# A gMLP and stick-breaking trunk in fp32r: two more pairs of columns five tile pairs wide, and a mixing in wider products

## The chip, the cores and the metric

The kernel runs on one core of a Trainium2 chip. Its engines are TensorE (PE in the profile, its weight loads PEld), VectorE (DVE), ScalarE (ACT), GpSimd (POOL) and SyncE (SP). The metric is the device time of one execution, in microseconds: the median of several runs. A profiled execution gives, beside its own time, a trace of every instruction.

## The reference

Two layers over a sequence of 256 tokens with 2048 channels (16 tiles of 128 channels, two tiles of 128 tokens).

```python
h = x
for i in range(DEPTH):                       # DEPTH = 2
    hn = rms_norm(h, norm_g[i])
    if i % 2 == 0:                           # layer a: gMLP, width 4096
        proj = hn @ a_w_in                   # 2048 x 12288: u | v | gate
        u, v = split(gelu(proj[:, :8192]));  zg = proj[:, 8192:]
        v = rms_norm(v, a_v_norm_g)
        mixed = tril(a_w_s) applied to v by chunks of 128 tokens, + a_b_s   # 16 groups of 256 channels
        y = (u * mixed * silu(zg)) @ a_w_out # 4096 x 2048
    else:                                    # layer b: stick-breaking attention, 16 heads of 128
        q, k, v, zg = split(hn @ b_w_in)     # 2048 x 8192
        y = (attention(q, k, v) * silu(zg)) @ b_w_out
    h = h + y
return rms_norm(h, final_g)
```

Nearly all arithmetic is in the four projections. All is float32.

## The kernel before, in words

**Split products.** A float32 factor is split into a high part in the type fp32r and a low part, the rest. A product then takes three matmuls: high by high, high by low, low by high (`terms`, L119 to L121). The left factor (activations, two token tiles) is split once and stays on chip. The weights come from memory, two k tiles (128x1024) at a time, and `cut` splits them: ScalarE copies the high part (L114), VectorE subtracts it for the low part (L115). Five pairs of such tiles can be in work (`wspl`).

**Pairs.** `Pair` computes two blocks of 512 columns at once. Of its k tiles, `ks` pairs are done with seven products of 2x2 blocks instead of eight (Winograd's form), the rest plainly in `column(0)` and `column(1)`. With k halves i and columns j the weights are tiles `b00`, `b01`, `b10`, `b11` in the program's names (b11, b12, b21, b22 in the code). The seven products are the blocks p1, p5, p6, p2, p7, p3, p4 in this order, each over `ks` tiles in groups of two (`qk0_p50` is block p5 of pair qk0, its first group). With `ks` = 5 the third group is a half one, of one tile (128x512): `p12`, `p52` and so on. Between the blocks VectorE forms differences and sums of the weight tiles (L275, L300), and POOL issues DMAs that add one tile onto another (`plus`, L280). The matching sums of the left factor are made once per layer by `sums`, for the fifth tile by `fifth`.

Before the change the v pairs (v0 to v6, layer a) and the first q/k pair (qk0, layer b) have `ks` = 4, as the gate/u pairs do (gu0 to gu7); the later pairs of layer b have 5. The fifth tiles of b00 and b01 lie in a pool of their own, those of b10 and b11 in the three buffers that also hold the loads of the plain columns (`wraw`).

**What sets the order.** The tile framework arranges each engine's instructions by its own estimate of time; the Python order, and a queue of small works that `tick` takes from, give it its input. Each engine then runs its list strictly in that order. A pair's second column is interleaved with the next pair's head: `run`, and by hand for the passage from o2 (the last pair of layer a's output) to qk0. All loads of weights are issued by SyncE (L221), in its order. In the text, the lead of a group is the time from the end of its low part's subtraction to the first product that reads it.

**The mixing** (`mixing`, one block of 512 v columns for each gu pair) splits the masked mixing matrix (`wh`, `wl`) and the normed v (`vh`, `vl`), and multiplies them by groups of 256 columns: for each token tile and group three products of 256 columns (L580 to L582), 12 in all, and a multiplication by the gain per token tile (L584).

**Attention's constants** are made when qk0 is under way: `mones`, `nu` and `one` by VectorE copies, `never` by a VectorE memset and a select on POOL; `n1_r`, layer b's norm factor, is computed on POOL too (L97).

Of the kernel before, what the change touches and what calls it, by code (L numbers as in the profile page):

```python
# [29 lines left out]
def trunk_kernel(ctx: ExitStack, tc: tile.TileContext, x, xt, gcols, wst, a_w_in, a_v_norm_g,  # L30
# [187 lines left out]

    def load(out, in_):

        ins = ins_of(nc.sync.dma_start(out, in_))  # L221
# [325 lines left out]
    with ExitStack() as lg:  # L547
# [5 lines left out]
        def mixing(b, pair):  # L553
# [15 lines left out]
            mixed[b] = []  # L569
            for t in range(NT):  # L570
                vh = pb.tile([P, CB], F32R, tag="vh", name=f"vh{b}_{t}")
                vl = pb.tile([P, CB], F32R, tag="vl", name=f"vl{b}_{t}")
# [1 line left out]
                nc.scalar.activation(vh, vs, AF.Identity, scale=rv[:, t:t + 1])
                nc.vector.scalar_tensor_tensor(vl, vs, rv[:, t:t + 1], f(vh), op0=ALU.mult, op1=ALU.subtract)
                mp = ps_ms.tile([P, CB], F32, tag="ms", name=f"mix{b}_{t}")
                for j in range(GPB):
                    o = mp[:, j * GD:(j + 1) * GD]
                    sl = slice(j * GD, (j + 1) * GD)
                    nc.tensor.matmul(o, wh[:, j, :], vh[:, sl], start=True, stop=False)  # L580
                    nc.tensor.matmul(o, wh[:, j, :], vl[:, sl], start=False, stop=False)
                    nc.tensor.matmul(o, wl[:, j, :], vh[:, sl], start=False, stop=True)  # L582
                ym = pa.tile([P, CB], F32, tag=f"ym{t}", name=f"ym{b}_{t}")
                nc.vector.tensor_mul(ym, mp, vg)  # L584
                mixed[b].append(ym)

        def evac_gu(b, j, t, bank):
            ym = mixed[b][t]
# [217 lines left out]
    nc.vector.tensor_copy(nu, scr2)  # L806
# [2 lines left out]
    nc.vector.memset(never, 0.0)
# [346 lines left out]
```

## Time and profile before

| | us |
|---|---|
| median of 3 runs (lowest to highest) | 1147.48 (1147.37 to 1147.52) |
| the profiled execution's own time | 1147.16 |
| its span, first to last instruction | 1145.4 |
| TensorE busy | 1134.8 (99%) |
| VectorE busy | 1006.3 (88%) |
| ScalarE busy | 816.6 (71%) |
| bytes moved | 263.69 MB, 230 GB/s on average |

A row of the timeline reads: start and duration in us, engine, line, operation, out<-in by the program's names without their numbers, shape, and in brackets how long the engine was idle before it and what ended that. `x3` is three instructions in one row. A row of the waits reads: who waited <- for whom, us in total, times, longest. Matmul durations overlap, so the cadence is read from starts. A row of the stretches gives busy time by engine, the granted clock of TensorE, the share of the DMA engines' time and the rate.

### The profile page before, as it was taken

What the parts mean: (1) busy time and instruction counts of PE and PEld (TensorE: products, weight loads), DVE (VectorE), ACT (ScalarE), POOL (GpSimd) and SP (SyncE); (2) the same over time, 40 slices, a digit from 0 to 9 for tenths busy, and PEclk for the clock granted to TensorE, in tenths of its full rate; (3) what the DMA queues carried; (4) which work ended last, traced back from release to release, by engine and by line L of the source; (5) the groups of instructions that cost most, each with busy time, mean ns of one, the idle gap of its engine ahead of it and who ended that gap; (6) DMA issues with size and microseconds to landing.
All of it is one profiled execution on the core that took longest, in us unless ns stands there. A gap on an engine that the chain in (4) does not pass through costs nothing.

```text
span 1145.4 us, 14888 instructions
## 1 busy us (share of the span) xinstructions
PE 1134.8 (99%) x5222; PEld 940.5 (82%) x5222; DVE 1006.3 (88%) x1108; ACT 816.6 (71%) x1072; POOL 94.5 (8%) x101
## 2 busy tenths in 40 slices
PE   9999999999999999999999999999999999999997
PEld 6788888888888888888888888888888888888885
DVE  7988888998999998987988679989889989897995
ACT  7777767767767767856657456788678877886574
POOL 0200010110110110100010000110100101100000
PEclk9999999999999999999999999999999999999999
DMA  9988787786787786677795768687787876837972
GB/s 330 319 274 250 194 262 256 195 270 231 204 258 241 212 257 224 182 236 203 254 270 171 266 201 284 170 268 208 184 283 199 211 228 173 273 87 241 334 225 82
DMA packets 135020, 263.69 MB, mean 230 GB/s; under 512 B 8864, under 2 KB 9376, under 8 KB 134816
## 3 DMA queue, kind: packets, MB, share of 16 engines
q1 hardware_dynamic: 117408, 227.57, 59.1%
q0 software_dynamic: 15728, 31.99, 15.6%
q10 hardware_dynamic: 1808, 3.17, 0.8%
q8 instruction: 41, 0.67, 0.2%
q14 instruction: 35, 0.29, 0.1%
HBM read 258.50 MB, written 4.19 MB: 229 GB/s over the span
## 4 chain that ended last, share of the span: by engine, by line
PE 96%; DMA 1%; ACT 1%; issue 1%; DVE 1%; SPq 0%; POOLq 0%; POOL 0%; ACTq 0%
PE gu_a L121 3%; PE gu_a L120 3%; PE gu_b L121 3%; PE gu_a L119 3%; PE gu_b L120 3%; PE gu_b L119 3%; PE gu_d L121 2%; PE op_acc L121 2%; PE gu_d L120 2%; PE op_acc L119 2%; PE op_acc L120 2%; PE gu_c L121 2%; PE gu_d L119 2%; PE gu_c L120 2%; PE gu_c L119 2%; PE qk_a L121 1%
## 5 line engine op out<-in xcount | busy, mean ns | idle before, releaser
L114 ACT CAST gu_p_hi<-gu_b 128x1024 fp32r<-128x1024 f32 x112 | 115.4, 1052 | 36.1 <-PE gu_c L121 19.7
L115 DVE TENSOR_TENSOR gu_p_lo<-gu_b,gu_p_hi 128x1024 fp32r<-128x1024 f32 x112 | 133.6, 1221 | 5.4 <-ACT gu_p_hi L114 4.9
L115 DVE TENSOR_TENSOR qk_p_lo<-qk_b,qk_p_hi 128x1024 fp32r<-128x1024 f32 (+1 forms) x77 | 80.8, 1075 | 8.3 <-ACT qk_p_hi L114 7.9
L114 ACT CAST gu_hi<-gu_raw 128x1024 fp32r<-128x1024 f32 x64 | 65.9, 1053 | 29.7 <-DMA gu_raw<-in_a_w_in 17.0
L115 DVE TENSOR_TENSOR gu_lo<-gu_raw,gu_hi 128x1024 fp32r<-128x1024 f32 x64 | 76.7, 1218 | 10.1 <-ACT gu_hi L114 10.1
L114 ACT CAST qk_p_hi<-qk_b 128x1024 fp32r<-128x1024 f32 (+1 forms) x77 | 70.4, 934 | 19.0 <-DMA qk_b<-in_b_w_in 4.6
L115 DVE TENSOR_TENSOR v_lo<-v_raw,v_hi 128x1024 fp32r<-128x1024 f32 (+1 forms) x41 | 48.4, 1193 | 21.2 <-ACT v_hi L114 21.0
L114 ACT CAST v_hi<-v_raw 128x1024 fp32r<-128x1024 f32 (+1 forms) x41 | 41.7, 1027 | 28.4 <-DMA v_raw<-in_a_w_in 26.3
L115 DVE TENSOR_TENSOR v_p_lo<-v_b,v_p_hi 128x1024 fp32r<-128x1024 f32 x42 | 50.2, 1220 | 3.3 <-ACT v_p_hi L114 3.1
L114 ACT CAST v_p_hi<-v_b 128x1024 fp32r<-128x1024 f32 x42 | 43.0, 1049 | 9.5 <-PE v_c L121 4.7
L115 DVE TENSOR_TENSOR bv_p_lo<-bv_b,bv_p_hi 128x1024 fp32r<-128x1024 f32 (+1 forms) x42 | 42.6, 1041 | 4.2 <-ACT bv_p_hi L114 4.0
L115 DVE TENSOR_TENSOR bg_p_lo<-bg_b,bg_p_hi 128x1024 fp32r<-128x1024 f32 (+1 forms) x42 | 42.4, 1040 | 4.1 <-ACT bg_p_hi L114 4.0
L114 ACT CAST o_p_hi<-o_b 128x1024 fp32r<-128x1024 f32 (+1 forms) x35 | 33.4, 966 | 16.6 <-PE op_acc L121 11.6
L114 ACT CAST bv_p_hi<-bv_b 128x1024 fp32r<-128x1024 f32 (+1 forms) x42 | 37.2, 908 | 9.6 <-DMA bv_b<-in_b_w_in 3.3
L114 ACT CAST bg_p_hi<-bg_b 128x1024 fp32r<-128x1024 f32 (+1 forms) x42 | 37.2, 907 | 7.9 <-DMA bg_b<-in_b_w_in 2.5
L114 ACT CAST op_hi<-op_raw 128x1024 fp32r<-128x1024 f32 x24 | 25.1, 1053 | 23.6 <-DMA op_raw<-in_a_w_out 10.5
L115 DVE TENSOR_TENSOR o_p_lo<-o_b,o_p_hi 128x1024 fp32r<-128x1024 f32 (+1 forms) x35 | 38.3, 1113 | 3.8 <-ACT o_p_hi L114 3.7
L114 ACT CAST o_hi<-o_raw 128x1024 fp32r<-128x1024 f32 x22 | 23.0, 1052 | 24.3 <-DMA o_raw<-in_a_w_out 23.2
L115 DVE TENSOR_TENSOR o_lo<-o_raw,o_hi 128x1024 fp32r<-128x1024 f32 x22 | 26.7, 1222 | 15.4 <-ACT o_hi L114 15.2
L280 POOL DMA_DIRECT2D gu_b<-in_a_w_in x16 | 19.7, 1228 | 237.7 <-DVE gu_b L275 202.2
L275 DVE TENSOR_TENSOR gu_b<-gu_b,gu_b 128x1024 f32<-128x1024 f32 x32 | 39.0, 1238 | 0.2
L114 ACT CAST qk_hi<-qk_raw 128x1024 fp32r<-128x1024 f32 x26 | 27.1, 1054 | 15.2 <-DMA qk_raw<-in_b_w_in 9.9
(773 smaller groups left out, 3820.0 us busy)
## 6 DMA issues: line engine op xcount, KB each, us to landing
gu_b<-in_a_w_in SPq DMA_DIRECT2D x64, 512.0 KB, 4.8
gu_raw<-in_a_w_in SPq DMA_DIRECT2D x64, 512.0 KB, 5.3
v_raw<-in_a_w_in SPq DMA_DIRECT2D x39, 512.0 KB, 6.0
qk_b<-in_b_w_in SPq DMA_DIRECT2D x32, 512.0 KB, 5.1
qk_raw<-in_b_w_in SPq DMA_DIRECT2D x26, 512.0 KB, 5.4
v_b<-in_a_w_in SPq DMA_DIRECT2D x24, 512.0 KB, 5.6
op_raw<-in_a_w_out SPq DMA_DIRECT2D x24, 512.0 KB, 5.4
o_raw<-in_a_w_out SPq DMA_DIRECT2D x22, 512.0 KB, 4.9
```

What stands on the lines that cost most here:

```text
L114: nc.scalar.copy(hi[:, sl], raw[:, sl])
L115: low[0] = nc.vector.tensor_sub(lo[:, sl], raw[:, sl], f(hi[:, sl]))
L119: nc.tensor.matmul(acc, lh, hi, start=first, stop=False, skip_group_check=True)
L120: nc.tensor.matmul(acc, lh, lo, start=False, stop=False, skip_group_check=True)
L121: nc.tensor.matmul(acc, ll, hi, start=False, stop=last, skip_group_check=True)
L275: nc.vector.tensor_sub(into[g], b0[g], b1[g])
L280: adds.append(nc.gpsimd.dma_start(into[g], self.src(HALVES[i][k], n, j), accum_op=ALU.add))
```

## The change

Three things are changed.

- The last v pair, v6, and the first q/k pair, qk0, take five tile pairs (`ks` = 5). For v6 all four fifth tiles get a pool of their own (`ex0`), so that none goes through `wraw` and POOL adds none of them twice; the sums for the fifth tile are made while v4 runs (`x_fifth`). For qk0 the fifth tiles of b00 and b01 lie in two buffers of the pool `jk` (`sg0`, `sg1`). Those hold, up to then, the full values and the sums from which layer b's own fifth sums are made (`xs1e`). A fifth tile is now always loaded right behind the load that precedes it in the program.
- The mixing's `vh`, `vl` and `ym` hold both token tiles, and a product covers both: six products of 512 columns for a block instead of 12 of 256. `vh` and `vl` have one buffer of twice the size instead of two.
- `mones`, `nu` and `one` are copied by ScalarE, `never` is cleared by POOL.

```diff
-KS_A = 4
+KS_A = 5
...
-    def load(out, in_):
+    def load(out, in_, behind=False):
         ins = ins_of(nc.sync.dma_start(out, in_))
+        if behind and not chain:
+            tc.add_manual_dep(ins, before[0], NOSYNC, reason="order of loads")
+        before[0] = ins.name
...
-                if i and g >= 2:
+                if i and g >= 2 and not roomy:
                     break
...
-                    raw = self.fifth(j, name)
-                load(raw, self.src(HALVES[i][k], n, j))
+                    raw = self.fifth(i, j, name)
+                load(raw, self.src(HALVES[i][k], n, j), g >= 2)
...
-            for g, (k, n) in list(enumerate(self.groups))[2:]:
+            for g, (k, n) in list(enumerate(self.groups))[len(tiles):]:
...
+    def x_fifth():
+        with tc.issue_after(ins_of(low[0])):
+            left.fifth(jk.tile([P, 2, 4, 1, P], F32R, tag="more", bufs=1, name="xs0e"), "s0e")
+
     def v_pair0(b):
-        p = Pair(columns(a_w_in, W + b * CB, W + (b + 1) * CB), left, KD, f"v{b}", KS_A,
-                 lambda j, t, bank: evac_v(b + j, t, bank))
-        return p
+        return Pair(columns(a_w_in, W + b * CB, W + (b + 1) * CB), left, KD, f"v{b}", KS_A if b == 6 else 4,
+                    lambda j, t, bank: evac_v(b + j, t, bank),
+                    mid=(lambda pair: queue.append((1, x_fifth))) if b == 4 else None)
...
-            mixed[b] = []
+            vh = pb.tile([P, NT, CB], F32R, tag="vh", bufs=1, name=f"vh{b}")
+            vl = pb.tile([P, NT, CB], F32R, tag="vl", bufs=1, name=f"vl{b}")
             for t in range(NT):
-                mp = ps_ms.tile([P, CB], F32, tag="ms", name=f"mix{b}_{t}")
-                for j in range(GPB):
-                    o = mp[:, j * GD:(j + 1) * GD]
-                    sl = slice(j * GD, (j + 1) * GD)
-                    nc.tensor.matmul(o, wh[:, j, :], vh[:, sl], start=True, stop=False)
-                    nc.tensor.matmul(o, wh[:, j, :], vl[:, sl], start=False, stop=False)
-                    nc.tensor.matmul(o, wl[:, j, :], vh[:, sl], start=False, stop=True)
-                nc.vector.tensor_mul(ym, mp, vg)
...
+            ym = mixed[b] = pa.tile([P, NT, CB], F32, tag="ym", name=f"ym{b}")
+            for j in range(GPB):
+                sl = slice(j * GD, (j + 1) * GD)
+                mp = ps_ms.tile([P, NT, GD], F32, tag="ms", name=f"mix{b}_{j}")
+                nc.tensor.matmul(mp, wh[:, j, :], vh[:, :, sl], start=True, stop=False)
+                nc.tensor.matmul(mp, wh[:, j, :], vl[:, :, sl], start=False, stop=False)
+                nc.tensor.matmul(mp, wl[:, j, :], vh[:, :, sl], start=False, stop=True)
+                nc.vector.tensor_mul(ym[:, :, sl], mp, vg[:, sl].unsqueeze(1).to_broadcast([P, NT, GD]))
...
+    def fifth(i, j, name):
+        return jk.tile([P, 1, CB], F32, tag=f"sg{j}", bufs=1, name=name)
...
-    p = Pair(columns(b_w_in, 0, D), left1, KD, "qk0", 4, lambda j, t, bank: evac_qk(0, j, t, bank),
-             mid=lambda pair: drain())
+    p = Pair(columns(b_w_in, 0, D), left1, KD, "qk0", KS_B, lambda j, t, bank: evac_qk(0, j, t, bank),
+             mid=lambda pair: drain(), fifth=fifth)
...
-    for _ in p.head():
-        next(tail)
+    for i, _ in enumerate(p.head()):
+        if i % 3 < 2:
+            next(tail)
...
-    nc.vector.tensor_copy(mones, scr[:, 0, :])
+    nc.scalar.copy(mones, scr[:, 0, :])
...
-    nc.vector.tensor_copy(nu, scr2)
+    nc.scalar.copy(nu, scr2)
...
-    nc.vector.memset(never, 0.0)
+    nc.gpsimd.memset(never, 0.0)
...
-    nc.vector.tensor_copy(one, ident)
+    nc.scalar.copy(one, ident)
```

**SyncE's loads of v6.** Before, as v4 ends (`v4_014` is the load of v4's k tiles 14 and 15 for column 0, `v6_b00_1` the second group of v6's tile b00):

```order
L221 DMA v6_b11_0_1165<-in_a_w_in 128x2x512
L221 DMA v6_b11_1_1167<-in_a_w_in 128x2x512
L221 DMA v6_b00_0_1100<-in_a_w_in 128x2x512
L221 DMA v6_b00_1_1102<-in_a_w_in 128x2x512
L221 DMA v4_014_raw_1076<-in_a_w_in 128x2x512
L221 DMA v4_18_raw_1119<-in_a_w_in 128x2x512
```

Now, from the first of the fifth tiles:

```order
L221 DMA v6_b10_2_1236<-in_a_w_in 128x512
L221 DMA v6_b01_0_1122<-in_a_w_in 128x2x512
L221 DMA v6_b01_1_1124<-in_a_w_in 128x2x512
L221 DMA v6_b01_2_1126<-in_a_w_in 128x512
L221 DMA v6_b11_0_1174<-in_a_w_in 128x2x512
L221 DMA v6_b11_1_1176<-in_a_w_in 128x2x512
L221 DMA v6_b11_2_1178<-in_a_w_in 128x512
L221 DMA v6_b00_0_1116<-in_a_w_in 128x2x512
L221 DMA v6_b00_1_1118<-in_a_w_in 128x2x512
L221 DMA v6_b00_2_1120<-in_a_w_in 128x512
L221 DMA v4_014_raw_1092<-in_a_w_in 128x2x512
L221 DMA v4_18_raw_1156<-in_a_w_in 128x2x512
```

Four loads of half tiles stand among v6's loads, all ahead of `v4_014`.

**SyncE and VectorE at the head of qk0.** SyncE, before, from the last load of o2 on, and now:

```order
L221 DMA o2_130_raw_6028<-in_a_w_out 128x2x512
L221 DMA qk0_08_raw_6221<-in_b_w_in 128x2x512
L221 DMA qk0_010_raw_6239<-in_b_w_in 128x2x512
L221 DMA qk0_012_raw_6257<-in_b_w_in 128x2x512
L221 DMA bv0_b00_2_6311<-in_b_w_in 128x512
```

```order
L221 DMA o2_130_raw_6011<-in_a_w_out 128x2x512
L221 DMA qk0_b00_2_5890<-in_b_w_in 128x512
L221 DMA qk0_b01_2_5896<-in_b_w_in 128x512
L221 DMA qk0_b10_2_6133<-in_b_w_in 128x512
L221 DMA qk0_b11_2_6163<-in_b_w_in 128x512
L221 DMA qk0_010_raw_6252<-in_b_w_in 128x2x512
```

VectorE at the same place, before and now:

```order
L115 TENSOR_TENSOR o2_126_lo_5966<-o2_126_raw_5963,o2_126_hi_5965 128x1024
L115 TENSOR_TENSOR qk0_p50_lo_5991<-qk0_b00_0_5916,qk0_p50_hi_5990 128x1024
L115 TENSOR_TENSOR o2_128_lo_6003<-o2_128_raw_6000,o2_128_hi_6002 128x1024
L300 TENSOR_TENSOR qk0_b00_0_5916<-qk0_b11_0_5981,qk0_b00_0_5916 128x1024
L115 TENSOR_TENSOR qk0_p51_lo_6019<-qk0_b00_1_5918,qk0_p51_hi_6018 128x1024
```

```order
L115 TENSOR_TENSOR o2_126_lo_5940<-o2_126_raw_5937,o2_126_hi_5939 128x1024
L115 TENSOR_TENSOR qk0_p12_lo_5956<-qk0_b00_2_5890,qk0_p12_hi_5955 128x512
L279 TENSOR_TENSOR qk0_b00_2_5890<-qk0_b01_2_5896,qk0_b00_2_5890 128x512
L115 TENSOR_TENSOR qk0_p50_lo_5974<-qk0_b00_0_5886,qk0_p50_hi_5973 128x1024
L304 TENSOR_TENSOR qk0_b00_0_5886<-qk0_b11_0_5962,qk0_b00_0_5886 128x1024
L115 TENSOR_TENSOR o2_128_lo_5986<-o2_128_raw_5983,o2_128_hi_5985 128x1024
```

The loads of the four half tiles take the place of the load of k=8; on VectorE the half group p12 and the difference of the half tiles stand between o2's k=26 and block p5.

**POOL at attention's constants**, before and now (`n1_r` is layer b's norm factor, the `qk0` rows are the accumulating DMAs):

```order
L280 DMA qk0_b01_1_5922<-in_b_w_in 128x2x512
L97 TENSOR_TENSOR n1_r_6074<-n1_ms_6072,half_84 128x2
L800 MEMSET scr_6085 128x256
L804 AFFINE_SELECT scr2_6090<-scr_6085 128x128
L810 AFFINE_SELECT never_6093<-never_6093 128x256
```

```order
L284 DMA qk0_b01_1_5894<-in_b_w_in 128x2x512
L284 DMA qk0_b01_2_5896<-in_b_w_in 128x512
L284 DMA qk0_b00_2_5890<-in_b_w_in 128x512
L814 MEMSET scr_6076 128x256
L823 MEMSET never_6084 128x256
L818 AFFINE_SELECT scr2_6081<-scr_6076 128x128
L824 AFFINE_SELECT never_6084<-never_6084 128x256
L97 TENSOR_TENSOR n1_r_6065<-n1_ms_6063,half_84 128x2
```

`n1_r` stood ahead of the constants and now stands behind them.

More of the change, by code (lines that the diff above doesn't have):

```diff
@@ L213, in trunk_kernel @@
     NOSYNC = mybir.DependencyInfo(mybir.DependencyClass.NoSync, mybir.DependencyReason.DATA)
-    chain = [None]
+    chain, before = [None], [None]
     def ins_of(x):
         return x.ins if hasattr(x, "ins") else x
-    def load(out, in_):
+    def load(out, in_, behind=False):
         ins = ins_of(nc.sync.dma_start(out, in_))
+        if behind and not chain:
+            tc.add_manual_dep(ins, before[0], NOSYNC, reason="order of loads")
+        before[0] = ins.name
         if chain:
@@ L231, in __init__ @@
         def __init__(self, src, left, nk, name, ks, evac, mid=None, fifth=None):
-            self.fifth = fifth or (lambda j, name: ex.tile([P, 1, CB], F32, tag=f"b1{j + 1}_2", name=name))
+            self.fifth = fifth or (lambda i, j, name: ex.tile([P, 1, CB], F32, tag=f"b{i + 1}{j + 1}_2", name=name))
             self.src, self.left, self.name, self.ks = src, left, name, ks
@@ L357, in trunk_kernel @@
     adds, pending, prior, ex = [], [], [], None
+    roomy = True
     def run(pair):
@@ L516, in trunk_kernel @@
             square(3 + 2 * i)
-    left.sums(max(KS_A, KS_GU), home("xs", [P, 2, 4, max(KS_A, KS_GU), P], F32R, "xs0"), "s0")
+    left.sums(4, home("xs", [P, 2, 4, 4, P], F32R, "xs0"), "s0")
     pending.append(p0.column(1))
     prior.append(KD // 4)
+    lx = ctx.enter_context(ExitStack())
+    ex = lx.enter_context(tc.tile_pool(name="ex0", bufs=1))
     for b in range(2, NV, 2):
@@ L522, in trunk_kernel @@
         chain.clear()
+    lx.close()
+    roomy = False
     yc = {}
@@ L568, in mixing @@
                 nc.vector.tensor_sub(wl, ws, f(wh))
[L569 removed]
+            vh = pb.tile([P, NT, CB], F32R, tag="vh", bufs=1, name=f"vh{b}")
+            vl = pb.tile([P, NT, CB], F32R, tag="vl", bufs=1, name=f"vl{b}")
             for t in range(NT):
[L571 to L572 removed]
                 vs = v_of(t, b * CB, CB)
[L574 to L585 removed]
+                nc.scalar.activation(vh[:, t], vs, AF.Identity, scale=rv[:, t:t + 1])
+                nc.vector.scalar_tensor_tensor(vl[:, t], vs, rv[:, t:t + 1], f(vh[:, t]), op0=ALU.mult, op1=ALU.subtract)
+            ym = mixed[b] = pa.tile([P, NT, CB], F32, tag="ym", name=f"ym{b}")
[6 more added lines that the diff above has]
+                nc.vector.tensor_mul(ym[:, :, sl], mp, vg[:, sl].unsqueeze(1).to_broadcast([P, NT, GD]))
         def evac_gu(b, j, t, bank):
[L588 removed]
+            ym = mixed[b][:, t]
             if j == 0:
```

2 lines of the change are left out of this document (removed).

## The prediction

> **What bounds the kernel now.** I read the page first: busy time by engine, then the chain of work that ended last.
>
> ```profile
> PE 1134.8 (99%) x5222; PEld 940.5 (82%) x5222; DVE 1006.3 (88%) x1108; ACT 816.6 (71%) x1072; POOL 94.5 (8%) x101
> PE 96%; DMA 1%; ACT 1%; issue 1%; DVE 1%; SPq 0%; POOLq 0%; POOL 0%; ACTq 0%
> ```
>
> TensorE is busy 99% of the span and carries 96% of the chain, so a product less is a gain and an added wait of TensorE is a loss. Next the waits of TensorE; this view has four rows, first and last shown (waited for, us, times, longest):
>
> ```profile
> PE wps L79 <- DVE warm L76: 1.3, 1, 1.3
> ...
> PE gT L420 <- ACT bsg L975: 0.2, 1, 0.2
> ```
>
> The four make 2.6 us, and none lies in the two pairs or the mixing that change. So the change has no wait to remove. What it can do is shorten TensorE's own stream, and what it can spoil is the lead with which the split weights arrive. Third, the stretches of the two pairs (columns: PE, PEld, DVE, ACT, POOL busy, granted clock, share of the DMA engines, GB/s):
>
> ```profile
> 99.90:117.00 17.10, 17.10 (x77) 14.17 (x76) 11.69 (x11) 10.40 (x15) 0.00 (x0) 1.00 0.96 325
> 140.00:180.00 40.00, 40.00 (x178) 33.15 (x177) 33.68 (x31) 28.29 (x38) 4.40 (x5) 1.00 0.84 246
> 676.00:680.00 4.00, 4.00 (x20) 3.30 (x19) 4.00 (x7) 1.86 (x2) 0.67 (x1) 1.00 0.16 61
> 680.00:690.00 10.00, 10.00 (x46) 8.29 (x45) 10.00 (x12) 7.12 (x8) 1.75 (x2) 1.00 0.89 196
> 700.00:710.00 10.00, 10.00 (x50) 8.37 (x49) 9.89 (x18) 10.00 (x16) 1.69 (x4) 1.00 0.99 353
> ```
>
> While v6's tiles are loaded (first row) the DMA engines are full, 0.96; in v6 itself (second) VectorE is idle 6.3 of 40 us. In qk0 VectorE is full, 10.00 and 9.89 of 10. So each widened pair stands where something beside TensorE has nothing to spare.
>
> **The gain.** With four tile pairs a pair of columns takes 7x4x3 + 8x4x3 = 180 products, with five 7x5x3 + 6x4x3 = 177. Two pairs save 6. The cadence of a product, and of the mixing's narrow ones, from the timeline of TensorE:
>
> ```profile
> 229.12 0.39 PE L119 MATMUL gu_c<-gu_p_hi,xs 128*128 128x512 f32 x1
> ...
> 230.48 0.39 PE L119 MATMUL gu_b<-gu_p_hi,xs 128*128 128x512 f32 x1
> ...
> 233.43 0.28 PE L580 MATMUL mix<-vh,wh 128*128 128x256 f32 x1
> ...
> 233.90 0.40 PE L120 MATMUL gu_d<-gu_p_lo,x_hi 128*128 128x512 f32 x1
> 234.13 0.40 PE L121 MATMUL gu_d<-gu_p_hi,x_lo 128*128 128x512 f32 x1
> ...
> 236.87 0.28 PE L582 MATMUL mix<-vh,wl 128*128 128x256 f32 x1
> ...
> 237.82 0.40 PE L120 MATMUL gu_a<-gu_lo,x_hi 128*128 128x512 f32 x1
> ```
>
> Six products of 512 columns start within 1.36 us (229.12 to 230.48), 0.227 each. The six saved give **-1.36 us**. The 12 narrow products of one block take 0.47 (four) + 0.95 (eight) = 1.42; six wide ones would take 1.36, 0.06 less, and each of two returns to the usual products (233.90 to 234.13) costs up to 0.01 that falls away. Over eight blocks that is **-0.6 us** (between -0.4 and -0.8), since 256 columns already cost hardly more than half of 512. The Trainium skill (TensorE: Matmul & The Clock Gate, Back-to-back issue gap) gives N/2.4 + 2.5 ns for a product by itself, 109 against 216; by that the mixing would gain an estimated 0.1 us. The same section's 131 ns for a stream at N=512 does not agree with the 0.227 here.
>
> The mixing's other parts cost nothing: as many multiplications and splits remain, and VectorE is ahead there:
>
> ```profile
> 233.24 3.49 DVE L115 TENSOR_TENSOR gu_lo<-gu_raw,gu_hi 128x1024 fp32r<-128x1024 f32 x3
> ```
>
> The first of these three low parts ends at 234.4 and is taken at 237.82 (row above), a lead of 3.4, which covers a multiplication that starts a product or two later. Without that cover it would cost 0.6 (one multiplication) in each block.
>
> **The load of v6, late for v4.** SyncE issues in order. The four new half tiles (4 x 256 KB = 1.05 MB) stand ahead of v4's load of k=14. What that load does now (timeline):
>
> ```profile
> 117.26 1.05 ACT L114 CAST v_hi<-v_raw 128x1024 fp32r<-128x1024 f32 x1 [6.68 <-DMA v_raw<-in_a_w_in]
> ...
> 118.34 1.23 DVE L115 TENSOR_TENSOR v_lo<-v_raw,v_hi 128x1024 fp32r<-128x1024 f32 x1 [5.77 <-ACT v_hi L114]
> ...
> 120.88 0.39 PE L120 MATMUL v_a<-v_lo,x_hi 128*128 128x512 f32 x1
> ```
>
> ScalarE waits 6.68 us for it, VectorE 5.77 us behind that; the low part is ready at 119.57 and TensorE takes it at 120.88, a lead of 1.31. At 325 GB/s the added 1.05 MB last 3.2 us; the 4% of this stretch in which the DMA engines are free could hide 0.7, so 2.5 to 3.2, and I take 2.7. TensorE stalls 2.7 - 1.31 = 1.4. In the new order VectorE then does ten operations of 1024 and two of 512 up to v4's k=10 (p10 to p12, two and a half differences, k=8, p50, p51, two sums, k=10): 10 x 1.14 + 2 x 0.60 = 12.6 (durations below), against 52 products, 11.8, of TensorE. The lead falls by another 0.8: **+2.2 us**, from +0.8 if half the transfer hides to +2.7. The 256 KB that the accumulating queue adds for v6 land long before block p7 reads them. v6's extra operations (seven half splits, two half differences and a half sum, less two splits of k=8: 10 x 0.60 - 2 x 1.14 = 3.7) lie in VectorE's 6.3 idle us; without them TensorE would wait up to 3.
>
> **qk0.** VectorE's part first. An operation of 128x1024 starts 1.14 after the one before it, one of 128x512 0.60 (rows below). Up to block p4's second group it gets six half splits and two half differences, 8 x 0.60 = 4.8, and the second pair of hT operations moves ahead of that point (0.79). The constants leave: 0.39 + 0.13 = 0.52. TensorE gets 6 x 3 x 0.227 = 4.1.
>
> ```profile
> 683.11 1.22 DVE L115 TENSOR_TENSOR o_lo<-o_raw,o_hi 128x1024 fp32r<-128x1024 f32 x1
> 684.25 1.22 DVE L115 TENSOR_TENSOR qk_p_lo<-qk_b,qk_p_hi 128x1024 fp32r<-128x1024 f32 x1
> ...
> 698.02 0.68 DVE L659 TENSOR_TENSOR h<-o_b,h 128x512 f32<-128x512 f32 x1
> 698.62 0.68 DVE L659 TENSOR_TENSOR h<-o_c,h 128x512 f32<-128x512 f32 x1
> ...
> 704.95 0.17 DVE L809 MEMSET never<- 128x128 uint32 x1
> ...
> 705.34 1.44 DVE L115 TENSOR_TENSOR qk_p_lo<-qk_b,qk_p_hi 128x1024 fp32r<-128x1024 f32 x1
> 706.71 0.22 DVE L806 CAST nu<-scr 128x128 fp32r<-128x128 f32 x1
> 706.84 0.86 DVE L683 SCALAR_TENSOR_TENSOR x<-hT,cols,x 128x256 fp32r<-128x256 f32 x2
> 707.63 1.21 DVE L115 TENSOR_TENSOR qk_p_lo<-qk_b,qk_p_hi 128x1024 fp32r<-128x1024 f32 x1
> ...
> 709.90 0.39 PE L120 MATMUL qk_d<-qk_p_lo,x 128*128 128x512 f32 x1
> ```
>
> The lead of that group is 709.90 - 708.84 = 1.06 now and 1.06 + 4.1 - 4.8 - 0.79 + 0.52 = 0.1 then. Nothing is left for a wait of VectorE, and the new order brings three. The loads they rest on (queue, KB each, median us from issue to landing):
>
> ```profile
> o_b<-in_a_w_out SPq DMA_DIRECT2D x1, 256.0 KB, 2.9
> ...
> o_b<-in_a_w_out POOLq DMA_DIRECT2D x1, 256.0 KB, 3.8
> ...
> bv_b<-in_b_w_in POOLq DMA_DIRECT2D x1, 256.0 KB, 5.1
> ...
> hs<-h ACTq DMA_DIRECT2D x1, 512.0 KB, 5.1
> ```
>
> and the timeline at the head of qk0, with the stretch after o2's last load:
>
> ```profile
> 673.76 6.76 SPq L221 DMA_DIRECT2D o_raw<-in_a_w_out  x2
> ...
> 686.38 1.05 ACT L114 CAST o_hi<-o_raw 128x1024 fp32r<-128x1024 f32 x1 [1.01 <-DMA o_raw<-in_a_w_out]
> ...
> 702.50 0.71 POOL L97 TENSOR_TENSOR n_r<-n_ms,half 128x2 f32<-128x2 f32 x1 [17.55 <-DVE n_ms L95]
> 704.66 0.31 POOL L800 MEMSET scr<- 128x256 f32 x1 [1.45 <-DMA hs<-h]
> ...
> 705.29 0.42 POOL L810 TENSOR_SCALAR_AFFINE_SELECT never<-never 128x256 bf16<-128x256 bf16 x1
> ```
>
> ```profile
> 686.30:688.00 1.70, 1.70 (x9) 1.39 (x9) 1.70 (x3) 1.54 (x2) 0.00 (x0) 1.00 1.04 316
> ```
>
> First, tile p12. Its load stands behind o2's last, which SyncE issued at 680.5 and which landed at 686.3. VectorE reaches p12 at 684.3 and would be done at 684.95. Its 256 KB follow at 316 GB/s: 0.8, so 687.1; ScalarE's and VectorE's halves end at 688.4: **a wait of 3.4**. If small loads could pass large ones it would land 2.9 after its issue, 683.4, and the wait is 0. Queued behind it on both engines are p50, o2's last two groups and all that follows.
>
> Second, p62 reads a half tile that POOL accumulates once p52 is split. Issue 0.2, landing 3.8 to 5.1, two halves 1.2: 5.2 to 6.5, while VectorE has 3 x 1.14 + 0.6 = 4.0 to do: 1.2 to 2.5, I take **1.2**.
>
> Third, n1_r now stands behind the constants on POOL, and these wait for the store of h. After that store is issued: 5.1, 0.2, constants 704.66 to 705.71 and one memset more, 1.05 + 0.3, n1_r 0.7, in all 7.35, and it is issued some 0.7 after h is complete; VectorE comes to r2q, which reads n1_r, 6.7 after h is complete (four groups of p2 and p7 at 1.14, a half group and the sum with es at 0.60, a hT pair at 0.79, 0.15 of small sums): 7.35 + 0.7 - 6.7 = **1.3**, from 0.8. ScalarE's copies of these constants wait for the same store and hold p72 and p3 behind them.
>
> TensorE stalls 3.4 + 1.2 + 1.3 - 0.1 = **+5.8 us**; with the lower ends 0 + 1.2 + 0.8 - 0.1 = 1.9. Moved to ScalarE, the constants are three short copies in that engine's idle time. Later pairs keep their order and regain the lead: in qk0's second column a split of 1.14 and 12 products of 0.227 are gone, and the next pair's groups are there to be split early.
>
> **Sum.** -1.36 - 0.6 + 2.2 + 5.8 = +6.0. The profiled execution took 1147.16 us (span 1145.4 and 1.8 around it), 0.3 below the runs' median 1147.48: 1147.16 + 6.0 = **1153.2 us**.
>
> **Rivals.** (1) *Loads pass each other.* The DMA engines are nearly idle before p12's load (share 0.16 at 676 to 680). The Trainium skill (DMA: Bandwidth & Descriptors, Queues, rings and completion order) says that each engine takes descriptors in ring order but that completion is not in order for the issuing engine; by its first half I get 687.1, by its second perhaps 683.4. Then qk0 costs 1.9, and with half of v6's transfer hidden 0.8: 1147.16 - 1.96 + 2.7 = 1147.9, no change. Against it: o2's load before it took 6.1 us itself, beside an accumulating transfer. (2) *All covered.* If p12 lands by 683.4, the accumulated half by 4.0 after p52, and v4's k=14 no more than 0.5 late, TensorE never waits and the 54 fewer products stand alone: 1145.2, just at faster. It decides at those three points; the full DMA engines in both stretches speak against it. (3) *The merged mixing waits.* One block's six products need both token tiles; if TensorE waits one multiplication of 0.60 in each of the eight blocks, 8 x 0.6 = 4.8 more than forecast, 1158.0. The lead of 3.4 there speaks against it; it decides once that lead is gone.
>
> **How the numbers follow.** Forecast 0.57, (1) 0.26, (2) 0.14, (3) 0.03. A difference under 0.2% (2.3 us) can't be told from none: faster is below 1145.2, slower above 1149.8. The forecast's own range is 1149.5 (one of the waits gone) to 1155.0 (upper ends of v6 and the accumulation). For 8 in 10 I go from 1146.0, which leaves (2) out, to 1155.0. Slower: forecast and (3), 0.60; same: (1) and a little of (2), which lies on the bound, 0.28; faster: the rest of (2), 0.12.
>
> **What would show it.** Right: TensorE's waits name v_lo or v_hi near 120 to 127 us (about 2 us) and qk_p_lo or qk_lo from 688 to 720 (5 to 6 us); VectorE idles over 3 us for qk_p_hi near 685, ScalarE waits on DMA qk_b there, and VectorE's r2q waits for POOL n_r. The mixing shows 48 products of 512 columns at 0.227. Wrong: TensorE's waits still make 2.6 us, p12's load lands within 3 us of its issue, or the products of 512 in the mixing are slower than two narrow ones.

## The result, and the profile after

The changed kernel takes 1154.49 us (median of 6 runs, 1152.92 to 1156.55), the kernel before beside it 1147.21 (6 runs): a ratio of 1.0066, interval 1.0053 to 1.0079. It is slower, and 1.3 us above the predicted 1153.2. Its profiled execution took 1154.21 us, span 1152.5.

Busy time and the chain of work, of the changed kernel's page:

```profile
PE 1137.5 (99%) x5168; PEld 938.0 (81%) x5168; DVE 1014.0 (88%) x1128; ACT 820.3 (71%) x1086; POOL 102.7 (9%) x105
PE 70%; DMA 12%; DVE 9%; issue 4%; ACT 4%; SPq 1%; POOL 0%; ACTq 0%; POOLq 0%; DVEq 0%
```

TensorE has 54 products less and is busy 2.7 us longer. It carries 70% of the chain, not 96%: the chain now runs back through loads and VectorE. The largest waits of TensorE, first six rows of eleven (the kernel before has four rows):

```profile
PE hT L426 <- DVE h L671: 1.5, 2, 1.4
PE wps L79 <- DVE warm L76: 1.3, 1, 1.3
PE yT L426 <- DVE yc L546: 1.0, 1, 1.0
PE v_acc L120 <- DVE v_lo L115: 0.7, 1, 0.7
PE f_acc L120 <- DVE f_lo L115: 0.5, 1, 0.5
PE v_acc L119 <- ACT v_hi L114: 0.5, 1, 0.5
```

**Where the time went** is read from the starts of the same product in both traces. Four such products of the kernel before (behind v4's k=12, at the head of the gate/u pairs, in the first layer's output, and in bv0, the pair behind qk0):

```profile
118.39 0.39 PE L120 MATMUL v_d<-v_lo,x_hi 128*128 128x512 f32 x1
...
180.26 0.39 PE L120 MATMUL gu_b<-gu_p_lo,xs 128*128 128x512 f32 x1
...
600.42 0.39 PE L120 MATMUL op_acc<-op_lo,yc 128*128 128x512 f32 x1
...
760.11 0.39 PE L120 MATMUL bv_a<-bv_lo,x 128*128 128x512 f32 x1
```

and the same four of the changed kernel:

```profile
118.15 0.39 PE L120 MATMUL v_d<-v_lo,x_hi 128*128 128x512 f32 x1
...
180.68 0.39 PE L120 MATMUL gu_b<-gu_p_lo,xs 128*128 128x512 f32 x1
...
601.20 0.39 PE L120 MATMUL op_acc<-op_lo,yc 128*128 128x512 f32 x1
...
766.13 0.39 PE L120 MATMUL bv_a<-bv_lo,x 128*128 128x512 f32 x1
```

The stretch with v6 grew by 0.6 us, that with the mixing by 0.4, that with qk0 by 5.2, and the rest to the end of the span by 1.0. The start of the first product itself differs by only 0.2. The stretch with the mixing holds a wait for yT (row above) behind a late load, and the rest one for f_lo. Both waits are in some of the traces of the experiments and not in others.

**qk0** is the place. Its stretches in the kernel before and in the changed one (columns as before: PE, PEld, DVE, ACT, POOL busy with their counts, clock, DMA share, GB/s):

```profile
690.00:705.00 15.00, 15.00 (x72) 12.52 (x71) 14.82 (x19) 10.96 (x16) 1.03 (x2) 1.00 0.78 268
705.00:712.00 7.00, 7.00 (x33) 5.79 (x32) 7.00 (x13) 5.14 (x8) 0.66 (x2) 1.00 0.95 337
```

```profile
690.00:705.00 15.00, 13.38 (x54) 9.91 (x54) 12.65 (x14) 7.28 (x10) 1.21 (x2) 1.00 0.40 88
705.00:712.00 7.00, 6.41 (x25) 5.32 (x26) 7.00 (x11) 6.00 (x13) 1.87 (x4) 0.76 0.68 197
```

The counts take in products in flight at an edge; by starts, TensorE begins 71 products of 512 columns in these 22 us instead of 93, and 22 of 0.227 are 5.0. Its idle time there is only 2.2 us: a product's row is 0.39 long where the next one starts 0.227 behind it, so a start that is up to 0.16 late shows no idle time, and the count tells more. The DMA engines, at 0.78 and 0.95 before, are at 0.40 and 0.68. The starts of TensorE show where the time is lost:

```profile
689.60 0.39 PE L119 MATMUL qk_e<-qk_p_hi,xs 128*128 128x512 f32 x1
690.09 0.50 PE L120 MATMUL qk_e<-qk_p_lo,xs 128*128 128x512 f32 x1
...
692.49 0.50 PE L120 MATMUL o_b<-o_lo,yc 128*128 128x512 f32 x1 [0.29 <-DVE o_lo L115]
...
703.09 0.50 PE L120 MATMUL qk_b<-qk_p_lo,xs1e 128*128 128x512 f32 x1 [0.22 <-DVE qk_p_lo L115]
```

Of the 5.9 us (5.2 and the saved 0.68) it loses 0.9 from 690.1 to 692.8, 0.8 at block p6's half group (702.4 to 703.4), 1.5 waiting for h at 705.42, 1.9 more up to 709.4 in a stretch at half the clock (last section), and 0.4 behind 712. The timeline of ScalarE and VectorE shows what stands in front:

```profile
686.83 1.57 ACT L114 CAST qk_p_hi<-qk_b 128x512 fp32r<-128x512 f32 x2 [6.60 <-DMA qk_b<-in_b_w_in]
687.48 0.69 DVE L115 TENSOR_TENSOR qk_p_lo<-qk_b,qk_p_hi 128x512 fp32r<-128x512 f32 x1 [4.85 <-ACT qk_p_hi L114]
...
701.69 1.57 ACT L114 CAST qk_p_hi<-qk_b 128x512 fp32r<-128x512 f32 x2 [5.50 <-DMA qk_b<-in_b_w_in]
702.34 0.69 DVE L115 TENSOR_TENSOR qk_p_lo<-qk_b,qk_p_hi 128x512 fp32r<-128x512 f32 x1 [2.24 <-ACT qk_p_hi L114]
...
713.08 0.17 DVE L804 TENSOR_SCALAR r2q<-n_r 128x2 f32<-128x2 f32 x1 [0.45 <-POOL n_r L97]
```

The three waits that the prediction named are there: p12's load (VectorE idle 4.85), the accumulated half tile of p62 (2.24), the norm factor (0.45). The DMA issues near 679 us (KB, us from issue to landing) show p12's load, the last row, behind a large load on its own queue and beside an accumulation:

```profile
qk_b<-in_b_w_in POOLq DMA_DIRECT2D x1, 512.0 KB, 8.9
o_raw<-in_a_w_out SPq DMA_DIRECT2D x1, 512.0 KB, 6.1
qk_b<-in_b_w_in SPq DMA_DIRECT2D x1, 256.0 KB, 7.9
```

### The profile page after: what moved, and what is told of

Its sections match the earlier page's. It is cut to its first block, busy times and chain, and to the rows that moved or that the text cites. A ratio compares the mean times of both kernels' runs of the same rounds, so it can differ in the third digit from the quotient of the medians.

```text
span 1152.5 us, 14839 instructions
## 1 busy us (share of the span) xinstructions
PE 1137.5 (99%) x5168; PEld 938.0 (81%) x5168; DVE 1014.0 (88%) x1128; ACT 820.3 (71%) x1086; POOL 102.7 (9%) x105
## 4 chain that ended last, share of the span: by engine, by line
PE 70%; DMA 12%; DVE 9%; issue 4%; ACT 4%; SPq 1%; POOL 0%; ACTq 0%; POOLq 0%; DVEq 0%
DMA f_raw<-in_b_w_out 3%; DMA gu_raw<-in_a_w_in 2%; PE gu_a L121 2%; PE gu_a L120 2%; PE gu_a L119 2%; DMA o_raw<-in_a_w_out 2%; PE op_acc L121 2%; PE op_acc L119 2%; PE op_acc L120 2%; PE gu_b L121 2%; PE gu_b L120 2%; PE gu_b L119 2%; DVE gu_p_lo L115 2%; PE gu_d L121 1%; PE gu_d L120 1%
## 5 line engine op out<-in xcount | busy, mean ns | idle before, releaser
L115 DVE TENSOR_TENSOR qk_p_lo<-qk_b,qk_p_hi 128x1024 fp32r<-128x1024 f32 (+1 forms) x84 | 85.0, 1041 | 15.9 <-ACT qk_p_hi L114 15.8
L114 ACT CAST qk_p_hi<-qk_b 128x1024 fp32r<-128x1024 f32 (+1 forms) x84 | 74.3, 906 | 30.9 <-DMA qk_b<-in_b_w_in 18.1
L115 DVE TENSOR_TENSOR v_lo<-v_raw,v_hi 128x1024 fp32r<-128x1024 f32 (+1 forms) x39 | 46.0, 1193 | 13.9 <-ACT v_hi L114 13.9
L115 DVE TENSOR_TENSOR v_p_lo<-v_b,v_p_hi 128x1024 fp32r<-128x1024 f32 (+1 forms) x49 | 54.5, 1144 | 4.1 <-ACT v_p_hi L114 3.8
L114 ACT CAST v_p_hi<-v_b 128x1024 fp32r<-128x1024 f32 (+1 forms) x49 | 47.2, 987 | 12.1 <-PE v_c L121 3.8
L121 PE MATMUL op_acc<-op_hi,yc 128*128 128x512 f32 x96 | 37.9, 395 | 0.0
```

The costliest lines, as they stand in the source:

```text
L114: nc.scalar.copy(hi[:, sl], raw[:, sl])
L115: low[0] = nc.vector.tensor_sub(lo[:, sl], raw[:, sl], f(hi[:, sl]))
L121: nc.tensor.matmul(acc, ll, hi, start=False, stop=last, skip_group_check=True)
```

## The experiments

On the three chips of the experiments single executions of the kernel before spread over 3.2 to 3.7 us (1145.6 to 1149.8 in all), so a ratio of medians tells about 1 us apart, and one trace less. In the table the columns are the ratio to the kernel before on the same chip, and from each trace, against the kernel before's, the growth of the four stretches between the products above: v6 (118.39 to 180.26), gate/u pairs with the mixing (to 600.42), qk0 (to 760.11), rest (to the end of the span). What lies ahead of 118.39 is left out; it differs by -0.9 to +1.2 between the traces. Where qk0 is unchanged its stretch is the same within 0.02, while the rest, in which no edit acts, differs by -0.3 to +2.4.

| kernel | ratio (interval) | v6 | mixing | qk0 | rest |
|---|---|---|---|---|---|
| the change | 1.0066 (1.0053 to 1.0079) | +0.6 | +0.4 | +5.2 | +1.0 |
| mixing alone | 0.9993 (0.9984 to 1.0002) | 0.0 | -0.8 | 0.0 | +2.4 |
| v6 alone | 1.0000 (0.9992 to 1.0009) | +0.1 | 0.0 | 0.0 | -0.3 |
| qk0 alone | 1.0061 (1.0049 to 1.0073) | 0.0 | 0.0 | +8.4 | -0.2 |
| change, qk0 at four | 0.9997 (0.9988 to 1.0007) | -0.6 | -0.6 | 0.0 | +0.6 |
| change, early fifth tiles | 1.0022 (1.0013 to 1.0031) | -0.1 | -0.4 | +2.4 | +0.3 |
| change, p52 first | 1.0057 (1.0044 to 1.0069) | -0.4 | +0.8 | +6.2 | +0.4 |
| change, both | 1.0016 (1.0006 to 1.0025) | +0.2 | -0.8 | +2.0 | -0.2 |
| qk0 at four, v6 early | 0.9989 (0.9980 to 0.9998) | -0.7 | -0.5 | 0.0 | +1.2 |
| change, all three repairs | 1.0006 (0.9996 to 1.0016) | -0.7 | -0.8 | +2.2 | +0.7 |
| the same, low parts left out | 0.9992 (0.9984 to 1.0001) | -0.7 | -0.5 | -0.5 | +0.3 |

**One part alone, and the change without qk0.** First the mixing by itself, the kernel before with

```diff
-                mp = ps_ms.tile([P, CB], F32, tag="ms", name=f"mix{b}_{t}")
+                mp = ps_ms.tile([P, NT, GD], F32, tag="ms", name=f"mix{b}_{j}")
...
+                nc.tensor.matmul(mp, wh[:, j, :], vh[:, :, sl], start=True, stop=False)
```

> The kernel before with the merged mixing alone (six products of 512 columns for a block, both token tiles in one product). Theory (the prediction's term): TensorE's stream is 0.6 to 0.7 us shorter and nothing waits, 1147.2 - 0.65 = 1146.6. Rival: the new wait of 1.0 us for yT near 498 us, which the changed kernel shows behind the gate/u pair's loads, belongs to the mixing and eats the gain: 1147.2 - 0.65 + 1.1 = 1147.7, and the wait is in its trace.

Measured 1146.91 (before 1147.66), 0.75 below (interval -1.8 to +0.2): the theory holds, the rival's 0.5 above is out. The trace is clearer than the times. The products at 180.26 and 600.42 of the kernel before start here at:

```profile
180.68 0.39 PE L120 MATMUL gu_b<-gu_p_lo,xs 128*128 128x512 f32 x1
...
600.00 0.39 PE L120 MATMUL op_acc<-op_lo,yc 128*128 128x512 f32 x1
```

0.42 late becomes 0.42 early: -0.84 us in eight blocks, with no wait for yT among TensorE's waits. That wait is in the traces of the change and of the kernel with p52 first at 1.0 and 1.2 us, in three others at 0.2 to 0.3, and in none of the rest. Of the nine traces with the new mixing it is in five, of the three without in none. So the mixing does not bring it every time; whether it makes it more likely, or it is only chance from one execution to the next, is not shown.

v6 by itself:

```diff
-KS_A = 4
+KS_A = 5
...
+        return Pair(columns(a_w_in, W + b * CB, W + (b + 1) * CB), left, KD, f"v{b}", KS_A if b == 6 else 4,
```

> The kernel before with v6 alone five tile pairs wide (its four fifth tiles loaded where the change loads them, ahead of v4's k=14); qk0, the mixing and attention's constants are as before. Theory: 0.7 saved, and TensorE waits 1.3 to 1.7 in v4's last k tiles: 1147.2 + 0.6 to 1.0 = 1148.0. Rival: v4's wait is part of what changes from one execution to the next, then 1147.2 - 0.7 = 1146.5. If the wait for yT near 498 us comes from v6 it adds 1.1 (1149.1).

Measured 1147.69 against 1147.66 (interval -0.9 to +1.0): on the median the saved 0.68 is lost again, no more. That lies between theory and rival and rules out neither. qk0 by itself:

```diff
-    p = Pair(columns(b_w_in, 0, D), left1, KD, "qk0", 4, lambda j, t, bank: evac_qk(0, j, t, bank),
-             mid=lambda pair: drain())
+    p = Pair(columns(b_w_in, 0, D), left1, KD, "qk0", KS_B, lambda j, t, bank: evac_qk(0, j, t, bank),
+             mid=lambda pair: drain(), fifth=fifth)
```

> The kernel before with qk0 alone five tile pairs wide (fifth tiles in the two buffers sg0 and sg1, tails of o2 given as in the change); v6, the mixing and attention's constants are as before. Theory: all of qk0's loss is made by qk0's own loads and operations: 0.7 saved and 6.0 waited, 1147.2 + 5.3 = 1152.5, and 1153.5 if the later wait of 1.0 near 1101 us follows from it. Rival: the constants on ScalarE and Pool make a large part (the norm factor behind them on Pool, ScalarE's copies behind the store of h); then this kernel loses less than 4 (under 1151.2).

Measured 1155.00, 7.3 above (5.6 to 8.4): all of the loss, so the rival (under 4) is out. VectorE waits in the same two places as in the changed kernel:

```profile
689.68 0.69 DVE L115 TENSOR_TENSOR qk_p_lo<-qk_b,qk_p_hi 128x512 fp32r<-128x512 f32 x1 [4.66 <-ACT qk_p_hi L114]
...
704.80 0.69 DVE L115 TENSOR_TENSOR qk_p_lo<-qk_b,qk_p_hi 128x512 fp32r<-128x512 f32 x1 [2.51 <-ACT qk_p_hi L114]
```

so the constants are not its cause. Their own price is not told apart from nothing: the sum of the three single parts, -0.7 + 0.0 + 7.3 = 6.6, differs from the change's 7.3 by less than the intervals. The change with qk0 at four tile pairs is the opposite test:

```diff
-    p = Pair(columns(b_w_in, 0, D), left1, KD, "qk0", KS_B, lambda j, t, bank: evac_qk(0, j, t, bank),
-             mid=lambda pair: drain(), fifth=fifth)
+    p = Pair(columns(b_w_in, 0, D), left1, KD, "qk0", 4, lambda j, t, bank: evac_qk(0, j, t, bank),
+             mid=lambda pair: drain())
```

> The changed kernel with qk0 back at four tile pairs (v6, the mixing and the constants as changed). Theory: -0.65 of the mixing, +0.6 to 1.0 of v6, nothing for the constants: 1147.2 to 1147.6; 1148.3 to 1148.7 if the wait for yT near 498 us comes again. Rival: the constants alone cost something, since Pool's norm factor stands behind them: over 1149.

Measured 1147.11, 0.5 below the kernel before (interval -1.4 to +0.8). The rival (over 1149, a price of the constants) is out.

**p12's load early.** The temporary values of layer b's fifth sums move out of the two buffers:

```diff
-                queue.append((1, lambda: left1.fifth(more("xs1e"), "xs1e")))
+                queue.append((1, lambda: left1.fifth(more("xs1e"), "xs1e", po.tile([P, 2, CB], F32, tag="h", bufs=3, name="xs1e_t"))))
```

> The changed kernel, but qk0's fifth tiles of b00 and b01 need not wait: the full values and sums of layer b's own fifth sums lie in a tile of the pool of h instead of sg0 and sg1, so that these two buffers are free when o2's block p4 is done, and SyncE loads the fifth tiles right behind qk0's b00_1 and b01_1, a dozen loads earlier. Nothing is left out. Theory: VectorE's wait of 4.85 us for p12 is gone, the accumulated half tile's 2.2 stays: the kernel before + 7 - 4 to 4.85 = before + 2.2 to + 3. Rival: VectorE's added work alone (4.8 us against a lead of 1.06) stalls TensorE and the late load only shows where; then the loss stays over + 4.5.

Measured 1150.33, 2.6 above the kernel before (1.5 to 3.6), against 7.3: the theory holds, and the late load cost some 4.7 (3 to 6.5, by the two intervals; 2.8 by qk0's stretch in the two traces, and 0.8 of the +2.4 that this one keeps is lost ahead of qk0, at 657). VectorE takes p12 without a wait, and keeps the wait for the accumulated half:

```profile
682.72 0.69 DVE L115 TENSOR_TENSOR qk_p_lo<-qk_b,qk_p_hi 128x512 fp32r<-128x512 f32 x1
...
697.54 0.69 DVE L115 TENSOR_TENSOR qk_p_lo<-qk_b,qk_p_hi 128x512 fp32r<-128x512 f32 x1 [2.22 <-ACT qk_p_hi L114]
```

**p52 first**, so that the accumulation has time:

```diff
+            turn = (2, 0, 1) if self.name == "qk0" else None
+            for g, _ in enumerate(self.block(self.b11, lambda k: left.sum_part(0, k), self.e, "p5", True, turn)):
+                if turn and g == 0:
+                    self.plus(self.b11, 1, 1, 2)
+                yield
```

> The changed kernel with block p5 of qk0 taken in another order, its half group (p52) first, so that Pool's accumulation onto that tile is issued two groups earlier and has some 8 us to land before p62 reads it; the late load of p12 stays. Nothing is left out. Theory: VectorE's wait of 2.2 us before p62 is gone, and with it h is complete earlier; p12's 4.85 stays: before + 7 - 2.2 = + 4.8, and + 3.6 if the stretch at half the granted clock (1.2 us) goes too. Rival: the accumulated half is on no path that counts: before + 6 to + 7.

Measured 1153.74, 6.0 above (5.0 to 7.9): the rival's figure, though not for its reason. The wait before p62 is gone, but the new order puts the late tile at the head of p5, and VectorE waits there four times:

```profile
688.37 0.69 DVE L115 TENSOR_TENSOR qk_p_lo<-qk_b,qk_p_hi 128x512 fp32r<-128x512 f32 x1 [5.10 <-ACT qk_p_hi L114]
689.49 0.69 DVE L283 TENSOR_TENSOR qk_b<-qk_b,qk_b 128x512 f32<-128x512 f32 x1 [0.43 <-DMA qk_b<-in_b_w_in]
690.95 0.69 DVE L115 TENSOR_TENSOR qk_p_lo<-qk_b,qk_p_hi 128x512 fp32r<-128x512 f32 x1 [0.76 <-ACT qk_p_hi L114]
691.89 1.23 DVE L115 TENSOR_TENSOR o_lo<-o_raw,o_hi 128x1024 fp32r<-128x1024 f32 x1 [0.26 <-ACT o_hi L114]
```

6.55 us in all instead of 4.85 + 2.24 + 0.45 = 7.54: one wait was traded for others. Both repairs together (the two edits above in one kernel):

> The changed kernel with both: the fifth tiles loaded early and p52 first. Theory: the two waits of VectorE made all of the loss; what stays is the changed kernel without qk0 (before - 0.5, measured) less three products (0.7) plus at most 0.5 for the norm factor: before - 1.2 to - 0.5. TensorE's clock stays at 1.00 around 705 us. Rival: VectorE's added work (4.8 us) stalls TensorE by itself: before + 2 to + 4.

Measured 1149.45, 1.8 above the kernel before (0.7 to 2.9). The theory (below it) is out; the rival (2 to 4 above) is within the interval at its lower end. The clock stays at 1.00 near 705 us, as the theory said. Of the 2.7 us that its trace still loses in qk0's stretch, half (1.3) is lost late, at 744; in qk0's seven blocks VectorE waits only 1.0 in all.

**v6's tiles earlier**, in the change with qk0 at four:

```diff
-            tc.add_manual_dep(ins, before[0], NOSYNC, reason="order of loads")
+            tc.add_manual_dep(ins, anchor["v4_b00_1"] if roomy else before[0], NOSYNC, reason="order of loads")
```

> The changed kernel with qk0 at four tile pairs, and v6's four fifth tiles loaded behind v4's last head tile, near 90 us, ahead of the stretch in which the DMA engines are full, instead of ahead of v4's k=14. Nothing is left out. Theory: v4's waits in its last k tiles come from that load: they vanish, and v6's three products show: before - 0.5 (measured without the early load) - 0.7 = before - 1.2. Rival: the waits come from VectorE's own added operations in v4 and v6: no difference, before - 0.5, and TensorE's waits still name v_lo and v_hi.

Measured 1146.45, 1.2 below the kernel before (interval 0.2 to 2.3): the only version shown faster than both kernels. The same kernel with late tiles was at -0.5, and the two intervals overlap, so here too the trace has to tell. The load of v4's k=14 comes earlier; ScalarE's row for it in the changed kernel, and then in this one:

```profile
118.70 1.05 ACT L114 CAST v_hi<-v_raw 128x1024 fp32r<-128x1024 f32 x1 [3.84 <-DMA v_raw<-in_a_w_in]
```

```profile
116.92 1.05 ACT L114 CAST v_hi<-v_raw 128x1024 fp32r<-128x1024 f32 x1 [6.35 <-DMA v_raw<-in_a_w_in]
...
118.00 1.23 DVE L115 TENSOR_TENSOR v_lo<-v_raw,v_hi 128x1024 fp32r<-128x1024 f32 x1 [3.56 <-ACT v_hi L114]
```

In all three traces with early tiles v6's stretch is shorter by 0.67 to 0.68, which is three products of 0.227. In the six with late tiles it lies between -0.6 and +0.6; that the loads fall differently in each execution is the likely reason, not a tested one.

**What is left.** All three repairs together:

> The changed kernel with all three repairs: qk0's fifth tiles loaded early, p52 first, v6's fifth tiles loaded near 90 us. Nothing is left out. Theory: the repairs add up: + 1.8 (measured with the first two) - 0.7 (v6) = before + 1.1. Rival: v4's wait was a part of what qk0's version lost by chance, then the gain is up to 2 and the time at or below before.

Measured 1147.90 against 1147.31: 0.6 above (interval -0.5 to 1.8), within the theory's reach and the rival's. Its trace still has +2.2 in qk0's stretch, that is 2.9 of waiting beside 0.68 saved, though VectorE idles only twice, by 1.0 in all, between 676 and 718:

```profile
685.21 0.69 DVE L115 TENSOR_TENSOR qk_p_lo<-qk_b,qk_p_hi 128x512 fp32r<-128x512 f32 x1 [0.76 <-ACT qk_p_hi L114]
...
686.17 1.23 DVE L115 TENSOR_TENSOR o_lo<-o_raw,o_hi 128x1024 fp32r<-128x1024 f32 x1 [0.27 <-ACT o_hi L114]
```

The starts of TensorE show where the 2.9 go. The largest gap in qk0's seven blocks is in front of p3's first group, 0.85 from start to start instead of 0.227; smaller ones of 0.1 to 0.2 stand in p2, p7 and p4. Another 0.6 is lost at 742, in qk0's second column, behind a half tile of the next pair (bv0) that VectorE waits 1.2 for:

```profile
709.10 0.50 PE L120 MATMUL qk_b<-qk_p_lo,xs 128*128 128x512 f32 x1 [0.45 <-DVE qk_p_lo L115]
```

```profile
737.97 0.69 DVE L115 TENSOR_TENSOR bv_p_lo<-bv_b,bv_p_hi 128x512 fp32r<-128x512 f32 x1 [1.19 <-ACT bv_p_hi L114]
```

Then the same kernel without the half groups' low parts:

```diff
+                if n == 1 and self.name == "qk0":
+                    hi = lo = wspl.tile([P, 2, CB], F32R, tag="hi", name=f"{self.name}_{nm}{g}_hi")
+                    nc.scalar.copy(hi[:, 0:1], b[g])
+                else:
+                    hi, lo = cut(b[g], n, f"{self.name}_{nm}{g}")
```

> The same with all three repairs, and the low parts of qk0's seven half groups left out: VectorE does not subtract them, and TensorE reads the high part in their place, so its products, the loads and ScalarE's copies stay (the sums of qk0 are then not the reference's). This takes 7 x 0.60 = 4.2 us of the 4.8 to 5.4 us that the widening adds to VectorE up to block p4. Theory: what the repairs leave of the loss, some 2.5 to 3 us of TensorE's waiting, is VectorE's added work: before + 1.1 - 2.5 = before - 1.4 or lower. Rival: what is left comes from the loads (o2's k=30 behind the fifth tiles, the DMA engines full from 705 us): then no more than 0.5 below the kernel with the three repairs, before + 0.6.

Measured 1146.04, 1.9 below the kernel with the repairs; by the two intervals that is some 0.3 to 3.4, so by the times alone the rival's 0.5 is not quite out. The trace is plainer: qk0's stretch falls by 2.6, to -0.5, as the theory has it. The stretch at the blocks p7 to p4, of the repaired kernel and then without the low parts:

```profile
705.00:712.00 7.00, 6.55 (x28) 4.72 (x27) 7.00 (x13) 6.17 (x9) 1.63 (x1) 1.00 0.98 356
```

```profile
705.00:712.00 7.00, 7.00 (x33) 5.79 (x32) 6.56 (x9) 6.70 (x10) 0.00 (x0) 1.00 1.02 364
```

With the DMA engines as full as before, VectorE gets 0.44 us free and TensorE's count is back at 33. The gap at 742 is gone too; how the low parts bear on it was not tried. So what the repaired loads leave of the loss, some 2 us in the seven blocks, is VectorE's own added work.

## Why the prediction came out right

The change is slower, and nearly all of it comes from qk0, as forecast. The sum was +6.0, the measured difference 7.3 (the ratio's interval makes it 6.1 to 9.1).

- **Six products, -1.36: right.** Where nothing waits, v6's stretch is 0.68 shorter, the half of it.
- **Mixing, -0.6 (-0.4 to -0.8): right in mechanism, a little too small.** -0.84 in the kernel that has it alone. The products of 512 start 0.227 apart and nothing waits for the second token tile; so rival (3) is out.
- **v6, +2.2 (0.8 to 2.7): the term was too large.** Its stretch grew by 0.64, so 1.3 of waiting in that execution, and 0.7 by the medians of the kernel with v6 alone (-0.2 to 1.7). The step that failed is the delay of v4's k=14, "I take 2.7": ScalarE took it at 118.70 instead of 117.26, 1.4 later. That the wait comes from this load is supported by the three traces with earlier tiles; the times do not show it.
- **p12's load, wait 3.4: right in mechanism, its time partly by luck.** Predicted were landing at 687.1 and VectorE's half done at 688.4; it landed at 686.7 and the half was done at 688.17. But o2's last load ahead of it landed at 684.5, not at 686.3, and p12's came 2.2 behind it, not 0.8; the two errors nearly cancel. VectorE idled 4.85 because it reached p12 at 682.63, not at 684.3. The sum also took VectorE's wait as TensorE's one for one: TensorE lost only 0.9 right behind it, and more at p62 and in the wait for h, by when the lead was spent. Rival (1), that a small load passes a large one, is out: 7.9 us from issue to landing, behind the large one; with it goes rival (2), that all is covered. The Trainium skill (DMA: Bandwidth & Descriptors, Queues, rings and completion order) states that each DMA engine takes descriptors in ring order; the trace agrees.
- **p62, 1.2 (to 2.5): VectorE idled 2.24,** near the upper end. What it costs TensorE by itself is not shown: with p12 late, taking p52 first gave 1.2, with p12 early 0.9, both within the intervals.
- **The norm factor, 1.3 (from 0.8): 0.45.** VectorE came to it 6.7 after h was complete, as assumed. Too large was the time on the other side: the store of h was issued 0.03 after h was complete, not 0.7 (the kernel before has 0.03 too), and n_r was done 7.05 after that, not 7.35.
- **A remaining lead of 0.1: wrong.** It was worked out at one group of p4 and took VectorE's added operations as nearly covered. With the loads repaired VectorE idles 1.0 us in qk0's seven blocks and TensorE still loses 2.9 (0.6 of it at 742, behind them); with 4.2 us of VectorE's operations gone it loses 0.2. The surplus costs some 2 us that the sum does not have. The group shortest of lead is p3's first, ahead of the group at which the lead was worked out.
- **Not foreseen:** the stretch at half the clock (below), and the waits for yT and f_lo, 1.0 and 0.5 in the profiled execution.

So the mechanism is right and the total partly luck: terms too large (v6 by 0.9 to 1.5, the norm factor by 0.8) stand against a term left out (VectorE's surplus). Of the signs named, VectorE's wait at 685, ScalarE's for DMA qk_b, r2q's for n_r came as said. TensorE's own waits did not: qk_p_lo was to be named with 5 to 6 us and is with 0.2 (hT with 1.5), and v_lo and v_hi with 2 us and are with 0.5, at 120.75 and 133.62. The loss shows in the count of products.

## What to carry to other kernels

A step that saves products is worth its saving only where the engine that prepares their operands has room: in qk0 0.7 us of TensorE were bought with 4.8 us of VectorE (the prediction's count) where the lead was 1.06. A small load issued behind a large one was here as late as that one and 2.2 us more, so tiles added to a full stretch belong ahead of it, in buffers that nothing late still holds. And where TensorE looks busy, count its products in a stretch before believing that it does not wait.

## What was not expected of the hardware

After h is complete the changed kernel's TensorE runs at half its clock. Rows of its timeline, then its stretches:

```profile
705.42 0.44 PE L426 MATMUL hT<-ident,h 128*128 128x128 f32 x2 [1.38 <-DVE h L671]
...
708.22 0.63 PE L119 MATMUL qk_a<-qk_p_hi,x 128*128 128x512 f32 x1
708.64 0.63 PE L120 MATMUL qk_a<-qk_p_lo,x 128*128 128x512 f32 x1
```

```profile
704.00:705.84 1.84, 0.46 (x3) 0.20 (x2) 1.84 (x4) 1.12 (x2) 0.00 (x0) 1.00 0.00 0
705.84:709.25 3.41, 3.25 (x12) 2.84 (x12) 3.41 (x5) 3.41 (x8) 0.00 (x0) 0.50 0.60 189
```

For 3.41 us the granted clock is 0.50 and products start 0.42 apart. The kernel with p52 first shows the same after a shorter gap, and the kernel with qk0 alone twice:

```profile
690.60:692.20 1.60, 1.01 (x3) 0.65 (x4) 1.00 (x2) 1.60 (x3) 1.17 (x2) 1.00 0.04 10
692.20:695.60 3.40, 3.40 (x9) 2.56 (x9) 3.37 (x4) 2.99 (x4) 0.59 (x1) 0.51 0.89 131
```

Nine products instead of 15 are 1.4 us of TensorE's time. What this adds to the total is not shown: VectorE was full in the same stretch (3.41 of 3.41), and of the changed kernel's six runs the one with the highest mean clock, 0.999, which leaves room for 3.5 us at half the clock at most in the whole run, took 1154.78, above the median. The Trainium skill (TensorE: Matmul & The Clock Gate, What's actually happening) gives a window of 3413 ns, which agrees with the length of the slow stretch, and an idle window of about 3.4 us as its cause. Such an idle window was not needed here: the longest gap before it was 1.4 us idle in one kernel and 1.1 in the other. The clock falls a second time in both traces, after the last product, at 1149.57 and at 1149.69; that is 130.0 and 134.0 times 3.413 us after the first fall (705.84 and 692.30), so these falls keep to one grid. A single gap of 1.0 at 498 us of the changed kernel, the wait for yT, left the clock at 1.00:

```profile
498.00:502.00 4.00, 3.45 (x17) 2.94 (x18) 4.00 (x6) 2.25 (x5) 0.00 (x0) 1.00 0.62 160
```

Whether what counts is how little TensorE does in one step of that grid was not tried. In the step that ends at 705.84 it is busy for 1.81 of 3.41 us, in the one that ends at 692.30 for 1.84, in the one with the wait for yT for 2.48; but near the end of the kernel with p52 first a step with 1.48 (1142.86 to 1146.27) left the clock at 1.00.
